# Moving 21 first-matrix tiles and 26 gathered rows ahead of the second-matrix stage, and splitting more tiles

## The chip, the cores and the metric

The kernel is one inference step of a small hybrid encoder, written for one Trainium2 chip and run on one of its cores. The metric is the device time in microseconds (us) of one execution. A core has engines that each run their own instruction queue strictly in order: TensorE (PE) multiplies matrices, VectorE (DVE) and ScalarE (ACT) do elementwise work, GpSimd (POOL) does elementwise work and starts indexed gathers, and SyncE (SP) starts the plain transfers. Sixteen DMA engines move the data of both kinds of transfers.

## What is computed

The reference runs one layer for two groups of tokens: 256 prompt tokens and 8 sequences of 16 sample tokens, 384 in all, each a row of 1024 numbers. Most of the layer (a modulated norm, an RWKV-7 branch, a sparse attention branch, gates) is done when the change begins to matter. Its last part is a product-key expert layer:

```python
x = x + g2 * _peer(h2, w_pq, peer_keys, peer_u, peer_v)

# inside _peer, for each block of 128 tokens hb:
q = (hb @ w_pq).reshape(128, 8, 2, 64)
s = einsum('nhpd,hpkd->nhpk', q, peer_keys)
...                                  # per head: 16 of 16384 experts e, softmax weights g
act = gelu(einsum('nhkd,nd->nhk', peer_u[e], hb))
return einsum('nhk,nhkd->nd', g * act, peer_v[e])
```

So each token picks 8 x 16 = 128 of 16384 experts. An expert has a row of `peer_u` and a row of `peer_v`, both of 1024 float32 numbers.

## The kernel before

The expert layer is computed in two ways at once, since they need different engines.

**The matrix way, for the 256 prompt tokens.** The 16384 experts are 128 tiles of 128. For each tile j, `dense_u(j)` (L1427) loads a 512 KB tile of `peer_u` (transposed; called `in_puT` in the profile), multiplies it with the tokens into the PSUM tile `fx`, and ACT writes the gelu of it: one late result of 128 x 256 numbers (128 KB). `dense_v(j)` (L1450) loads the 512 KB tile of `peer_v` (`in_pv`) and multiplies the weighted late result with it, adding into four PSUM banks (`bx`, `cp`, and two `dx`). In between, every late result must be multiplied by the tokens' expert weights, a matrix that is zero for the experts that a token did not pick. The stage that builds this matrix is `weights` (L1343): 2 x 32 steps, in each of which DVE and ACT make one-hot factors (`oh`), TensorE multiplies them four times, and the product is multiplied into tiles 0 to 75 where they lie (`G` and `G2`, L1367; DVE in one step, POOL in the next) while its columns for tiles 76 to 127 go to DRAM (`wst`, L1368, L1370) and come back later as `Ws` (L1484).

**Splitting.** A float32 product is either done whole on the float32 data, or as three products of parts: ACT rounds the tile to a high part (`wh`), DVE subtracts to get the low part (`wl`), and TensorE multiplies high x high, high x low, low x high. This is `split` (L1419) and `hilo` (L225). The u tiles 0 to 35 are whole, the others split. In the v stage every third tile is whole (L1453), and a split one also needs its late result split into `Gh` and `Gl`.

**The gather way, for the 128 sample tokens.** `peer_sparse` (L1508) is a Python generator. POOL gathers 128 rows (one per token, 512 KB in all) of `peer_u` or `peer_v` into one of five `raw` buffers (L1518). DVE multiplies a u gather with the tokens and sums (L1529), or adds a v gather times its coefficient to `acc` (L1539). The groups are 4 u gathers, one gelu, 4 v gathers; 256 gathers in all. Each call of `pull(rate)` adds `rate` to a counter and issues two gathers for each whole number in it; in the v stage a gather also waits for the v tile five places earlier (L1660, L1520).

**Order.** The stages follow in program text: whole u tiles, then split u tiles up to 75, then `weights` with `ahead` called after each of its 64 steps, then the loop over the 128 v tiles. A scheduling pass then fixes the order of instructions on each engine; nothing is reordered at run time. Tiles 76 to 127 have no place of their own in the kept results: the first NB of them are written to DRAM (`gO`, L1447) and loaded back (`gB`, two buffers, L1458) when their v tile comes; the others stay in NA = 12 buffers (`gA`). What is not yet done when the v stage begins is done inside it (L1662).

```python
N1, NW, NA, NB = 36, 76, 12, 20                          # L180
SR, UR = (0.5, 0.4, 0.69), 0.5                           # L181
def ahead(n):                                            # L1636
    un[0] += UR
    if todo and un[0] >= 1 and (todo[0] < NW + NB or todo[0] < NW + NB + NA - 1):
        un[0] -= 1
        u = todo.pop(0)
        gs[u] = self.dense_u(u)
    pull(SR[1])
order = sorted(range(128), key=lambda j: (j + 0.5) / NW if j < NW else (j - NW + 0.5) / (128 - NW) + 0.06)
for n, j in enumerate(order):                            # L1659
    pull(SR[2])
    while todo and sum(u >= NW + NB for u in gs) < NA - 1:
        u = todo.pop(0)
        gs[u] = self.dense_u(u)
    self.dense_v(j, gs.pop(j) if j >= NW else self.kept(j), out, n)
```

The key of `order` spreads tiles 76 to 127 evenly among the others. All tiles of `peer_u` and `peer_v`, `Ws`, and `gB` are loaded by SP's queue, in its order; the `w` tiles have four buffers, `wh` four, `wl` three.

Of the kernel before, what the change touches and what calls it, by code (L numbers as in the profile page):

```python
# [176 lines left out]
ORDER = "GGIRRDMMMGRMRDMRGMGGMRMDGMMRRMGDMMMGGGGGGMGGM"  # L177


N1, NW, NA, NB = 36, 76, 12, 20  # L180
SR, UR = (0.5, 0.4, 0.69), 0.5  # L181
S0, PH = 30, 4
WB, EB = (4, 4, 3), 5
UENG, VENG, GENG, VN = 'v', 'v', 'g', 3
SENG = 'gv'
HENG, EENG, OB = 'va', 'vg', 3

# [1510 lines left out]
```

## Time and profile before

| | |
|---|---|
| median of 3 runs | 1863.67 us (1856.91 to 1869.19) |
| profiled execution: its time, its span | 1860.99 us, 1859.2 us |
| mean granted TensorE clock | 0.96 |
| TensorE busy | 1740.9 us (94%) |
| VectorE busy | 1379.4 us (74%) |
| ScalarE, GpSimd busy | 693.3 us (37%), 724.1 us (39%) |
| moved by DMA | 434.11 MB, mean 233 GB/s |

From the trace: the last split u tile of `G2` ends at about 1219 us, the steps of `weights` run from there to about 1364 us, the first v product starts at 1361 us, and the last v product ends at about 1850 us. The rest is the residual and its store.

In the windows quoted below a row gives a stretch of the span, then for PE, PE's weight loads, DVE, ACT and POOL the busy time and in brackets the number of instructions, then the granted clock, the busy share of the DMA engines, and what they moved in GB/s. Group rows read: line, engine, operation, output<-input, size, count | busy time, mean ns of one | idle time before them and what ended it. A float32 product appears as two PE records, one of the split parts as one. Wait rows read: engine and line, what it waited for, total us, times, longest us.

### The profile page before, as it was taken

The page shows a single profiled execution, that of the slowest core. Times are in us where ns is not written, and L with a number is a line of the kernel's source. Part 1 is how long each engine was busy: PE and PEld are TensorE (multiplying, and loading weights), DVE is VectorE, ACT ScalarE, POOL GpSimd, SP SyncE. Part 2 cuts the span into 40 slices and gives each one's busy share as a digit, 9 for nine tenths or more (in the row PEclk, how much of TensorE's full clock was granted, in tenths as well). Part 3 has the DMA queues.
Part 4 walks back from the last instruction along what each step waited for, and adds up shares of the span by engine and source line. Part 5 has one row for each costly group of instructions (what it writes and reads, how often), then busy time and mean ns, then how long its engine had stood idle before and what let it go on. Part 6 is the DMA issues. An engine that isn't in the chain of part 4 may idle for free. (4 is left out here: it accounts for less than half of the span.)

```text
span 1859.2 us, 33617 instructions
## 1 busy us (share of the span) xinstructions
PE 1740.9 (94%) x12621; PEld 1436.3 (77%) x12621; DVE 1379.4 (74%) x2905; ACT 693.3 (37%) x1402; POOL 724.1 (39%) x763
## 2 busy tenths in 40 slices
PE   7997999999999989899988979999999888999998
PEld 4985888877877867798877869999975556776765
DVE  4549678767767745445999999899967777787773
ACT  4432333333243333334221135478842222333332
POOL 2331333223223210024255566563346676465541
PEclk8996999999999989899998989999999999999999
DMA  8421563454264274655487969975489999999994
GB/s 307 141 79 34 168 224 91 147 168 137 78 218 137 70 243 151 213 174 179 148 313 284 359 244 331 383 291 182 164 294 369 375 374 356 351 373 344 347 344 157
DMA packets 181083, 434.11 MB, mean 233 GB/s; under 512 B 39348, under 2 KB 78388, under 8 KB 180920
## 3 DMA queue, kind: packets, MB, share of 16 engines
q1 hardware_dynamic: 144056, 297.73, 46.8%
q0 software_dynamic: 36864, 134.23, 19.3%
q8 instruction: 99, 1.62, 0.3%
q14 instruction: 64, 0.52, 0.1%
HBM read 401.65 MB, written 30.24 MB: 232 GB/s over the span
## 5 line engine op out<-in xcount | busy, mean ns | idle before, releaser
L231 DVE TENSOR_TENSOR wl<-w,wh 128x1024 fp32r<-128x1024 f32 x278 | 351.2, 1269 | 138.5 <-PE mm L223 64.3
L227 ACT ACTIVATE wh<-w 128x1024 fp32r<-128x1024 f32 x282 | 295.3, 1053 | 221.6 <-PE mm L223 88.0
L223 PE MATMUL fx<-h2h,wl 128*128 128x256 f32 x736 | 214.3, 291 | 10.4 <-DVE wl L231 10.3
L1518 POOL DMA_INDIRECT raw<-in_pu,pe x128 | 161.9, 1265 | 154.5 <-DVE acc L1539 46.6
L223 PE MATMUL fx<-h2h,wh 128*128 128x256 f32 x736 | 215.6, 293 | 4.3 <-ACT wh L227 3.2
L1518 POOL DMA_INDIRECT raw<-in_pv,pe x128 | 169.8, 1327 | 121.0 <-PE dx L223 45.4
L223 PE MATMUL fx<-h2l,wh 128*128 128x256 f32 x736 | 209.8, 285 | 0.0
L1539 DVE SCALAR_TENSOR_TENSOR acc<-raw,dots,acc 128x1024 f32<-128x1024 f32 x127 | 169.8, 1337 | 17.9 <-DMA raw<-in_pv,pe 16.7
L1529 DVE SCALAR_TENSOR_TENSOR raw<-raw,sh 128x1024 f32<-128x1024 f32 x128 | 163.4, 1291 | 17.1 <-DMA raw<-in_pu,pe 16.7
L223 PEld LDWEIGHTS fx<-h2h,wl 128*128 128x128 f32 x736 | 140.1, 190 | 14.4 <-DVE wl L231 12.7
L223 PEld LDWEIGHTS fx<-h2h,wh 128*128 128x128 f32 x736 | 140.9, 191 | 10.1 <-ACT wh L227 4.5
L223 PE MATMUL fx<-h2f,w 128*128 128x256 f32 x576 | 133.5, 394 | 14.4 <-ACT G L1445 14.4
L223 PEld LDWEIGHTS fx<-h2l,wh 128*128 128x128 f32 x736 | 140.4, 191 | 2.1 <-issue 1.7
L223 PEld LDWEIGHTS fx<-h2f,w 128*128 128x128 f32 x576 | 112.9, 198 | 33.3 <-ACT G L1445 16.4
L223 PE MATMUL mm<-LTh,wh 128*128 128x384 f32 (+1 forms) x344 | 121.9, 355 | 1.7 <-ACT wh L227 1.0
L223 PE MATMUL mm<-LTl,wh 128*128 128x384 f32 (+1 forms) x344 | 120.7, 351 | 1.2 <-POOL LTl L477 1.2
L223 PE MATMUL mm<-LTh,wl 128*128 128x384 f32 (+1 forms) x344 | 121.0, 352 | 0.0
L223 PE MATMUL mm<-wh,LTh 128*128 128x256 f32 (+1 forms) x360 | 105.4, 293 | 0.6 <-ACT qx L876 0.6
L223 PE MATMUL mm<-wh,LTl 128*128 128x256 f32 (+1 forms) x360 | 104.6, 291 | 0.0
L223 PE MATMUL mm<-wl,LTh 128*128 128x256 f32 (+1 forms) x360 | 104.4, 290 | 0.0
L1367 POOL TENSOR_TENSOR G<-G,wg 128x144 f32<-128x144 f32 (+1 forms) x64 | 61.7, 988 | 85.6 <-ACT wg L1364 85.5
L223 PEld LDWEIGHTS mm<-wh,LTh 128*128 128x128 f32 x360 | 70.1, 195 | 4.6 <-issue 2.7
(549 smaller groups left out, 4193.3 us busy)
## 6 DMA issues: line engine op xcount, KB each, us to landing
w<-in_puT SPq DMA_DIRECT2D x128, 512.0 KB, 6.1
w<-in_pv SPq DMA_DIRECT2D x128, 512.0 KB, 6.8
w<-in_w_in SPq DMA_DIRECT2D x70, 512.0 KB, 4.5
w<-in_w_ada SPq DMA_DIRECT2D x48, 512.0 KB, 4.2
cKT<-in_cKT SPq DMA_DIRECT2D x32, 256.0 KB, 4.2
cV<-in_cV SPq DMA_DIRECT2D x32, 256.0 KB, 4.5
w<-in_w_pq SPq DMA_DIRECT2D x16, 512.0 KB, 3.6
d<-wst SPq DMA_DIRECT2D x8, 832.0 KB, 4.3
```

What stands on the lines that cost most here:

```text
L223: return self.nc.tensor.matmul(out, l, r, start=start, stop=stop, skip_group_check=True, **kw)
L227: self.nc.scalar.activation(hi, src, AF.Copy)
L231: (self.nc.vector if eng == "v" else self.nc.gpsimd).tensor_tensor(lo, src, hi, op=OP.subtract)
L1367: (nc.vector if w is p else nc.gpsimd).tensor_tensor(g, g, w[:, :, c0:c1], op=OP.mult)
L1518: d = nc.gpsimd.indirect_dma_start(out=u, out_offset=None, in_=src, in_offset=bass.IndirectOffsetOnAxis(ap=e[:, j:j + 1], axis=0))
L1529: nc.vector.scalar_tensor_tensor(u, u, 1.0, h2, op0=OP.mult, op1=OP.mult, accum_out=dots[:, j:j + 1])
L1539: nc.vector.scalar_tensor_tensor(acc, v, dots[:, j:j + 1], acc, op0=OP.mult, op1=OP.add)
```

## The change

Only tables of numbers change:

```diff
-N1, NW, NA, NB = 36, 76, 12, 20
-SR, UR = (0.5, 0.4, 0.69), 0.5
+N1, NW, NA, NB = 36, 76, 12, 41
+SR, UR = (0.5, 0.62, 0.55), 0.82
 S0, PH = 30, 4
 WB, EB = (4, 4, 3), 5
-UENG, VENG, GENG, VN = 'v', 'v', 'g', 3
+UENG, VENG, GENG, VN = 'v', 'v', 'g', 5
```

`UR` is the rate at which `ahead` takes up u tiles: 64 steps x 0.5 = 32, of which the limit in `ahead` lets 31 through; 64 x 0.82 = 52.48, so all 52. `NB` = 41 sends 41 of the 52 late results through DRAM and leaves 11 in the `gA` buffers. `SR[1]` and `SR[2]` are the rates of `pull` beside the steps of the matrix and beside the v tiles: 26 more gathers now stand in the weights stage, and as many fewer in the v stage. `VN` = 5 makes every fifth v tile whole: 26 whole tiles, not 42, so 16 more are split.

The order of the instructions, read from the built programs. First VectorE in the weights stage, from the 1841st row of its queue on. `wl` is the low part of a u tile, `oh` the one-hot factors, `G` the kept results multiplied by the matrix, `acc` and `raw` the work on gathered rows. Before:

```order
L1539 SCALAR_TENSOR_TENSOR acc_11650<-raw_15415,dots_15338,acc_11650 128x1024
L1354 TENSOR_TENSOR oh_13568<-wA_13431,wB_13432 128x512
L1402 TENSOR_TENSOR oh_13568<-pT_2137_11034,dx_13148 128x512
L231 TENSOR_TENSOR wl_13468<-w_13464,wh_13467 128x1024
L1367 TENSOR_TENSOR G_11261<-G_11261,mm_13509 128x4x36
L1367 TENSOR_TENSOR G_2273_11729<-G_2273_11729,mm_13509 128x4x40
L1354 TENSOR_TENSOR oh_13585<-wA_13431,wB_13432 128x512
L1539 SCALAR_TENSOR_TENSOR acc_11650<-raw_15418,dots_15338,acc_11650 128x1024
L231 TENSOR_TENSOR wl_13538<-w_13534,wh_13537 128x1024
```

The same place now:

```order
L1539 SCALAR_TENSOR_TENSOR acc_11650<-raw_15339,dots_15115,acc_11650 128x1024
L1354 TENSOR_TENSOR oh_13689<-wA_13507,wB_13508 128x512
L1402 TENSOR_TENSOR oh_13689<-pT_2137_11034,dx_13148 128x512
L231 TENSOR_TENSOR wl_13416<-w_13412,wh_13415 128x1024
L1529 SCALAR_TENSOR_TENSOR raw_15449,dots_15448<-raw_15449,sh_2254_11648 128x1024
L1367 TENSOR_TENSOR G_11261<-G_11261,mm_13624 128x4x36
L1367 TENSOR_TENSOR G_2273_11729<-G_2273_11729,mm_13624 128x4x40
L1354 TENSOR_TENSOR oh_13742<-wA_13507,wB_13508 128x512
L1539 SCALAR_TENSOR_TENSOR acc_11650<-raw_15342,dots_15115,acc_11650 128x1024
L231 TENSOR_TENSOR wl_13476<-w_13472,wh_13475 128x1024
L1529 SCALAR_TENSOR_TENSOR raw_15452,dots_15448<-raw_15452,sh_2254_11648 128x1024
```

Rows of `raw` work stand between the steps where there were none. In the whole stage from its 1823rd row to the first `Gl`, VectorE had 4 rows of `acc` and none of `raw`, with 33 of `wl`; now it has 16 of `acc`, 14 of `raw` and 54 of `wl` (three of each `wl` count belong to the first v tiles). The gathered rows all lie in the first 30 of the 62 rows that multiply `G`; the later part holds one-hot factors and `wl` alone.

Second, SP's queue in the later part of the v stage. `w` is a loaded tile, `Ws` four tiles' columns of the weight matrix, `gB` a late result from DRAM. Before, from row 717:

```order
L1484 DMA Ws_18571<-d_11262 128x8x128
L1416 DMA w_17459<-in_puT 128x1024
L1416 DMA w_17492<-in_pv 128x1024
L1416 DMA w_17521<-in_pv 128x1024
L1416 DMA w_17527<-in_pv 128x1024
L1416 DMA w_17556<-in_puT 128x1024
L1416 DMA w_17589<-in_pv 128x1024
L1416 DMA w_17619<-in_pv 128x1024
L1416 DMA w_17628<-in_puT 128x1024
```

Now, from row 733:

```order
L1484 DMA Ws_17916<-d_11262 128x8x128
L1416 DMA w_17643<-in_pv 128x1024
L1458 DMA gB_17746<-d_11263 128x256
L1416 DMA w_17671<-in_pv 128x1024
L1416 DMA w_17698<-in_pv 128x1024
L1416 DMA w_17712<-in_pv 128x1024
L1458 DMA gB_17800<-d_11263 128x256
L1416 DMA w_17740<-in_pv 128x1024
L1416 DMA w_17765<-in_pv 128x1024
```

The 512 KB loads of u tiles are gone from this stretch, and 128 KB loads of late results stand there instead. No u tile is left in SP's queue, or in TensorE's, after the first v product. Ahead of the weights stage, up to the 1845th row of VectorE's queue, the kinds of instructions stand in the same order as before.

## The prediction

> **What bounds the kernel now.** I read the stretches of the last stages first, then the prices of single instructions, the waits of the queues, and last what the DMA engines moved. The rows are the end of the split u tiles, the weights stage, three parts of the v stage, and below them a stretch inside the weights stage.
>
> ```profile
> span 1859.2 us, 33617 instructions
> 1100.00:1219.00 119.00, 116.51 (x959) 115.11 (x960) 109.95 (x138) 58.61 (x105) 69.35 (x47) 1.00 0.95 357
> 1219.00:1364.00 145.00, 142.88 (x1213) 141.64 (x1211) 136.59 (x207) 124.98 (x299) 59.45 (x62) 1.00 0.55 194
> 1364.00:1550.00 186.00, 166.48 (x554) 106.64 (x554) 137.13 (x174) 47.05 (x77) 120.16 (x102) 0.96 0.99 370
> 1550.00:1800.00 250.00, 242.96 (x1140) 182.38 (x1141) 191.26 (x237) 86.76 (x132) 134.05 (x104) 0.99 0.95 353
> 1800.00:1850.00 50.00, 50.00 (x185) 34.45 (x183) 25.81 (x31) 16.31 (x26) 5.07 (x4) 1.00 0.63 213
> 1255.00:1273.00 18.00, 18.00 (x157) 18.00 (x156) 17.50 (x28) 15.86 (x39) 6.79 (x8) 1.00 0.50 175
> ```
>
> In the weights stage TensorE never pauses (18.00 of 18.00) and VectorE hardly does; the DMA engines are half idle. The v stage, 486 us, has two halves. Up to 1550 it has no u tile; the DMA engines are full (0.99, 370 GB/s) and TensorE waits. From 1550 on the 21 u tiles come in, TensorE is busy 97% and the DMA engines 95%. So the change takes work from a stage limited by loads, then by loads and TensorE together, and puts it into one limited by TensorE and VectorE.
>
> **Prices on TensorE.** Pieces of the chain that ended last, with start, length and count of records; here they follow each other without a gap:
>
> ```profile
> 1576.73 2.88 PE fx L223 x24
> 1572.38 0.92 PE dx L223 x4
> 1715.16 0.86 PE cp L223 x2
> 1716.02 1.72 PE dx L223 x4
> ```
>
> A u tile is 24 records of 0.12 us, 2.88 us. A split v tile is 12 records of 0.23 (0.92 / 4), 2.76 us. A whole one is 8 records of 0.43, 3.44 us. A one-hot record comes out of the 18 us row: the order puts 64 of them beside eight steps, so 157 records are 64 and 93 of u tiles; 18.00 - 93 x 0.12 = 6.84, / 64 = 0.107, and a product has two.
>
> **The change, stage by stage.** *Weights stage.* TensorE gets 21 u tiles, 21 x 2.88 = +60.5 us, and there was no gap to take them. That is the lower bound. VectorE gets 21 `wl` and 26 gathered rows, and the order (above) puts those rows into the first half of the stage, where VectorE will be late and TensorE will wait; after the last of them TensorE still has many u tiles to do alone. Groups of VectorE in the weights stage, then three of the stretch 1150 to 1219, where gathers run:
>
> ```profile
> L231 DVE TENSOR_TENSOR wl<-w,wh 128x1024 fp32r<-128x1024 f32 x34 | 45.3, 1334 | 6.2 <-ACT oh L1407 2.8 <-ACT wst L1368 1.1 <-issue 1.0
> L1354 DVE TENSOR_TENSOR oh<-wA,wB 128x512 f32<-128x512 f32 x55 | 38.7, 729 | 0.1
> L1367 DVE TENSOR_TENSOR G<-G,mm 128x160 f32<-128x160 f32 (+1 forms) x62 | 27.2, 481 | 0.0
> L1402 DVE TENSOR_TENSOR oh<-pT,dx 128x512 f32<-128x512 f32 x27 | 18.3, 679 | 0.0
> L1539 DVE SCALAR_TENSOR_TENSOR acc<-raw,dots,acc 128x1024 f32<-128x1024 f32 x4 | 5.4, 1352 | 0.0
> L1394 DVE TENSOR_TENSOR wB<-wab,clate 128x512 bf16<-128x512 bf16 x6 | 4.5, 758 | 0.0
> L1393 DVE TENSOR_TENSOR wA<-wA,pT 128x256 f32<-128x256 f32 x6 | 3.7, 621 | 0.0
> L1391 DVE TENSOR_TENSOR wA<-wab,clate 128x256 f32<-128x256 bf16 x6 | 2.8, 466 | 0.1
> ...
> L1539 DVE SCALAR_TENSOR_TENSOR acc<-raw,dots,acc 128x1024 f32<-128x1024 f32 x14 | 18.0, 1285 | 1.8 <-DMA raw<-in_pv,pe 1.6
> L1529 DVE SCALAR_TENSOR_TENSOR raw<-raw,sh 128x1024 f32<-128x1024 f32 x15 | 17.8, 1219 | 1.8 <-DMA raw<-in_pu,pe 1.8
> L1529 DVE DVE_READ_ACCUMULATOR raw<-raw,sh 128x1 f32 x14 | 1.1, 82 | 0.0
> ```
>
> I follow VectorE from its 1823rd row (the first multiplication of `G` after the last split u tile) to its 1972nd, a `wl` soon after the last gathered row, and from there TensorE. Busy time by count: 34 `G` at 0.439 (27.2 / 62) 14.9, 29 `oh` at 0.704 20.4, 14 at 0.678 9.5, 26 `wl` at 1.332 34.6, 16 `acc` at 1.286 20.6, 14 `raw` at 1.27 (1.19 and 0.08 to read the sum) 17.7, 17 small ones at about 0.5, 8.6; together 126 us. The groups overlap a little: the eight groups shown and 3 us of smaller ones add to 149 us where the window says 136.6 busy, a factor of 0.916, which leaves 116 us. Behind that `wl` TensorE still has 622 records of u tiles and 108 one-hot products, 622 x 0.12 + 108 x 0.213 = 97.6 us. The path is 213 us. Before, the same start gives 3.5 us for a first `wl` and then TensorE throughout, 718 x 0.12 + 220 x 0.213 = 133 us, 136.5 us.
>
> ```profile
> 1220.10 0.94 DVE L1367 TENSOR_TENSOR G<-G,mm 128x160 f32<-128x160 f32 x2
> L223 PE MATMUL bx<-w,G x52: 590/591/669, 1361.2 to 1827.3; 128*128 128x512 f32 x52
> ```
>
> From that start to the first v product it took 141 us, 3% more. So **+77 us**, with the 3% **+79**; I take +78. It can't be below +60.5; above, the landing of rows may show. In the v stage VectorE waited this long for rows, 65 of them:
>
> ```profile
> DVE raw L1529 <- DMA raw<-in_pu,pe: 10.7, 4, 3.5
> DVE acc L1539 <- DMA raw<-in_pv,pe: 5.7, 4, 3.8
> ```
>
> (16.4 us in 186, so 26 rows at that price are 7 us), and each group of four stops VectorE for a gelu by ACT, which is busy 125 of 145 us here; with twice those 7 us the upper end is +92.
>
> Taken at nothing in this stage: 21 more stores of late results on SP, 21 `wh` and 21 gelus on ACT, 26 gathers on POOL.
>
> ```profile
> SPq L1447 <- ACT gO L1445: 45.2, 17, 4.7
> POOL G L1367 <- ACT wg L1364: 85.5, 27, 9.5
> L227 ACT ACTIVATE wh<-w 128x1024 fp32r<-128x1024 f32 x34 | 36.2, 1065 | 6.0 <-PE fx L223 4.4 <-DMA w<-in_pv 1.4
> L1445 ACT ACTIVATE gO<-fx 128x256 f32<-128x256 f32 x20 | 7.7, 384 | 0.0
> L1518 POOL DMA_INDIRECT raw<-in_pv,pe x16 | 23.6, 1477 | 13.7 <-DVE raw L1529 8.8 <-issue 3.0 <-DVE acc L1539 1.8
> ```
>
> SP waits on a store for its gelu, 2.7 us at a time (45.2 / 17), and the next u loads stand behind it; four `w` buffers and half-idle DMA engines cover that. If they did not, 21 x 2.7 = 57 us would be at stake, but 20 such stores cost TensorE nothing that shows in the 18.00 row. ACT goes from 125 to about 155 us (21 x 1.45) in a stage that grows to over 215; POOL's 85.5 us of idle time holds 26 gathers of 1.5 us.
>
> *v stage.* What the DMA engines moved from 1364 to 1850, with its issues, then from 1364 to 1550, and one of VectorE's groups from 1364 to 1850:
>
> ```profile
> DMA packets 59818, 167.54 MB, mean 345 GB/s; under 512 B 5361, under 2 KB 21233, under 8 KB 59790
> w<-in_puT SPq DMA_DIRECT2D x21, 512.0 KB, 6.9
> gB<-d SPq DMA_DIRECT2D x20, 128.0 KB, 7.1
> raw<-in_pu,pe POOLq DMA_INDIRECT x76, 8.0
> raw<-in_pv,pe POOLq DMA_INDIRECT x76, 8.0
> DMA packets 28896, 68.73 MB, mean 370 GB/s; under 512 B 2329, under 2 KB 13994, under 8 KB 28887
> L231 DVE TENSOR_TENSOR Gl<-gA,Gh 128x256 fp32r<-128x256 f32 x22 | 9.3, 422 | 14.9 <-ACT Gh L227 14.8
> ```
>
> 21 u tiles and 26 gathers of 0.524 MB go, 24.6 MB; 21 late results of 0.131 MB come, 2.8 MB: 145.7 MB remain. TensorE loses 60.5 us of u tiles and 16 x (3.44 - 2.76) = 11 us by splitting, and has 26 x 3.44 + 102 x 2.76 = 371 us left. VectorE had 137 + 191 + 26 = 354 us; 26 gathered rows (at 1.28) and 21 `wl` (at the 1.33 above) go, 16 `wl` and 16 `Gl` (0.42 each) come: about 320. So the loads are the longest, as in the first half. At its 370 GB/s, all but the last five tiles and the results (3.1 MB) take 142.6 / 0.370 = 385 us; some ten split tiles are then still to be multiplied, 28 us. 413 us, **-73**. Bounds: at the 353 GB/s of the second half 404 + 28 = 432, -54; if loads never bound, TensorE at the 0.96 clock of the first half, 371 / 0.96 = 386 and about 4 us to the first product, -96. I take the first half's rate, since the stage now has its mix throughout: gathers, v tiles and late results, no u tile.
>
> The Trainium skill ("DMA: Bandwidth & Descriptors", section "Where 436 GB/s comes from") has two ceilings: about 358 GB/s for a core's transfers from HBM, and 435 for the fabric of the on-chip memory. By the one the stage would take 142.6 / 0.358 + 28 = 426 us and save 60, which ends at 1882, the edge of my forecast's own range; by the other TensorE would bind, which is rival B. The measured 370 GB/s over 186 us lies above the first and far from the second, so I take neither.
>
> *Sum*: +78 - 73 = **+5 us** on the profiled 1861 us, 1866. The median of the runs shown is 2.7 us above the profiled execution; so I forecast **1868 us**, no change that counts: a measurement of this kernel can tell about 1% (19 us).
>
> **The rivals.**
>
> *A, slower: late results come too late.* A reloaded late result must land (7.1 us), be multiplied by POOL behind its gathers, and only then can ACT round it; ACT's queue has the next tiles' `wh` behind that.
>
> ```profile
> ACT Gh L227 <- POOL gB L1464: 39.1, 9, 7.6
> L1464 POOL TENSOR_TENSOR gB<-gB,Ws 128x256 f32<-128x256 f32 x20 | 20.2, 1015 | 2.1 <-DMA modr<-d 1.4 <-DVE raw L1529 0.4
> ```
>
> 20 of them cost ACT 39.1 us; 21 more at the same price, uncovered, are +41, so 1868 + 41 = 1909. Against it: these 39.1 us lie in the 186 us where the DMA engines were full anyway. They came one per 9.3 us there and will come one per about 8 (41 over some 105 tiles of 3.2 us). With two buffers it decides once one result holds its buffer for over 16 us; landing, multiplying and the `Gl` take 8.5 (7.1 + 1.0 + 0.4), and ACT's part and the queueing would have to add as much again. Chance 0.12.
>
> *B, faster: the v stage becomes TensorE's.* With the u tiles gone the queues may be fed better than at 370 GB/s. Then it saves 90 to 96, and with VectorE keeping up better in the weights stage, +68 (between 60.5 and 78): 1864 + 68 - 93 = 1839. For it, 357 GB/s at 0.95 up to 1219 is 376 at full share; against it, 0.99 is as full as the engines get. Chance 0.12.
>
> *C, slower: the weights stage stumbles.* VectorE, ACT and TensorE are all near full there, and rows that land late stop VectorE in its order: +92, with the v stage as forecast, 1864 + 92 - 73 = 1883. Chance 0.10.
>
> That the change does not do what it says is ruled out by the order, which has no u tile after the first v product.
>
> **How the numbers follow.** My forecast has 0.66, with its own range of 1852 to 1882. Faster by over 1% (below 1845): B, 0.12. Slower by over 1% (above 1882): A, most of C, 0.20. Within 1%: the rest, 0.68. The range must leave out no more than 0.2: it takes in B and C and leaves out A, 1840 to 1890.
>
> **What would show it.** In the profile after: the stretch from the first row after 1219 to the first v product some 220 us long, with TensorE pausing in its first half, not in its second; from there to the end of the products about 413 us, DMA share 0.97 or more nearly to the end, and TensorE near 90% throughout. A stage of 205 us would show that VectorE's rows cost nothing (towards B). DMA shares of 0.9 in the v stage, with ACT waiting on POOL's `gB` for over 80 us, would be A. The forecast fails if the two stages don't change by nearly the same amount.

## The result, and the profile after

The changed kernel takes 1877.12 us (median of 8 runs, 1872.7 to 1886.76) against 1861.66 us for the kernel before (8 runs): a ratio of 1.0089, 95% interval 1.0067 to 1.011. It is 15 us slower, below the 1% that was called no change, and 9 us above the forecast of 1868. As a change it is +15 us where the forecast had +5: the 1868 us stood on the 1863.67 us that the kernel before had in its first three runs, 2 us above its median here. One of the 12 runs of experiment 5 was slow, 1880.52 us; the median there has it in, the ratio leaves it out.

The same starts and ends as in the prediction, read in the timeline: from VectorE's first multiplication of `G` after the last split u tile to the first v product, and from there to the end of the last v product. In after the three instructions are (start, length, engine, line, operation):

```profile
1220.34 0.93 DVE L1367 TENSOR_TENSOR G<-G,mm 128x160 f32<-128x160 f32 x2
...
1442.87 1.02 PE L223 MATMUL bx<-w,G 128*128 128x512 f32 x2
...
1866.19 0.63 PE L223 MATMUL dx<-wh,Gl 128*128 128x512 f32 x2
```

| | weights stage | v stage | sum |
|---|---|---|---|
| before | 141 | 489 | 630 |
| forecast | 220 | 413 | 633 |
| after | 222.5 | 424 | 646.5 |

So the change put 81.5 us into the first stage (forecast 78) and took 65 out of the second (forecast 73). The prediction counted the v stage of before from 1364 us on, 486 us; from the first v product, as here, it is 489, so that its 413 us would be 76 less, and its two stages together +3, not +5. The profiled execution of after took 1876.63 us, 15.6 more than that of before.

The first line of the page of after:

```profile
span 1874.7 us, 33942 instructions
```

Stretches of the last stages of after, with the columns as before (PE, PEld, DVE, ACT, POOL, granted clock, DMA share, GB/s); the first two are the weights stage in halves, the next three the v stage while it is loaded, in halves and whole, the last its end:

```profile
1219.00:1325.00 106.00, 93.94 (x759) 92.46 (x758) 104.60 (x148) 70.86 (x159) 68.63 (x57) 0.97 0.88 314
1325.00:1443.00 118.00, 114.92 (x962) 114.75 (x961) 85.67 (x124) 83.68 (x185) 21.40 (x32) 0.99 0.54 185
1443.00:1630.00 187.00, 173.78 (x641) 119.66 (x639) 149.17 (x185) 62.45 (x98) 105.82 (x84) 0.99 0.98 363
1630.00:1820.00 190.00, 171.50 (x623) 118.54 (x624) 157.90 (x188) 63.73 (x98) 110.92 (x92) 0.97 0.96 351
1443.00:1820.00 377.00, 345.29 (x1264) 238.20 (x1263) 307.07 (x372) 126.18 (x195) 216.74 (x175) 0.98 0.97 357
1820.00:1866.00 46.00, 45.90 (x177) 32.75 (x176) 29.95 (x39) 17.47 (x27) 7.55 (x6) 1.00 0.70 252
```

The weights stage has two unlike halves now. In the first VectorE is full (104.60 of 106) and TensorE pauses for 12 us; in the second TensorE pauses for 3 us and VectorE for 32. Three groups of VectorE over the whole stage, from 1219 to 1443, suggest why:

```profile
L231 DVE TENSOR_TENSOR wl<-w,wh 128x1024 fp32r<-128x1024 f32 x54 | 68.2, 1264 | 30.2 <-issue 15.2 <-ACT oh L1407 8.0 <-ACT wst L1368 3.7
...
L1539 DVE SCALAR_TENSOR_TENSOR acc<-raw,dots,acc 128x1024 f32<-128x1024 f32 x16 | 21.0, 1315 | 0.1
L1529 DVE SCALAR_TENSOR_TENSOR raw<-raw,sh 128x1024 f32<-128x1024 f32 x15 | 19.0, 1273 | 0.0
```

The gathered rows (`acc` and `raw`, 40 us) have no idle time before them: VectorE went from one to the next. In the v stage the DMA engines are at 0.97, not 0.99, and move 357 GB/s, not the 370 that the forecast took. What they moved from 1443 to 1866, and three waits from 1443 to 1820 (who, for whom, total us, times, longest):

```profile
DMA packets 56219, 146.13 MB, mean 345 GB/s; under 512 B 4961, under 2 KB 23521, under 8 KB 56195
```

```profile
PEld bx L223 <- ACT wh L227: 31.7, 21, 3.8
...
ACT Gh L227 <- POOL gB L1464: 23.5, 7, 5.9
PE bx L223 <- ACT wh L227: 23.1, 18, 3.4
```

The bytes are as forecast (145.7 MB). ACT waits for late results, 23.5 us in all, with the next tile's `wh` queued behind, and TensorE waits 23.1 us for `wh`. Whether one causes the other, and both the lower rate, is what the experiments had to say.

### The profile page after: what moved, and what is told of

Read it like the earlier page. It is cut to its first block, busy times and chain, and to the rows that moved or that the text cites. A ratio compares the mean times of both kernels' runs of the same rounds, so it can differ in the third digit from the quotient of the medians.

```text
span 1874.7 us, 33942 instructions
## 1 busy us (share of the span) xinstructions
PE 1742.6 (93%) x12685; PEld 1451.3 (77%) x12685; DVE 1410.6 (75%) x2937; ACT 716.9 (38%) x1434; POOL 729.4 (39%) x763
## 5 line engine op out<-in xcount | busy, mean ns | idle before, releaser
L231 DVE TENSOR_TENSOR wl<-w,wh 128x1024 fp32r<-128x1024 f32 x294 | 373.4, 1275 | 138.6 <-PE mm L223 60.5
L227 ACT ACTIVATE wh<-w 128x1024 fp32r<-128x1024 f32 x298 | 311.3, 1054 | 200.9 <-PE mm L223 82.3
L1518 POOL DMA_INDIRECT raw<-in_pu,pe x128 | 166.4, 1300 | 184.0 <-PE dx L223 69.0
L1367 POOL TENSOR_TENSOR G<-G,wg 128x144 f32<-128x144 f32 (+1 forms) x64 | 54.8, 879 | 103.8 <-ACT wg L1364 103.5
L227 ACT ACTIVATE Gh<-G 128x256 fp32r<-128x256 f32 x62 | 25.8, 418 | 130.1 <-PE dx L223 118.2
```

The source lines that it names most:

```text
L227: self.nc.scalar.activation(hi, src, AF.Copy)
L231: (self.nc.vector if eng == "v" else self.nc.gpsimd).tensor_tensor(lo, src, hi, op=OP.subtract)
L1367: (nc.vector if w is p else nc.gpsimd).tensor_tensor(g, g, w[:, :, c0:c1], op=OP.mult)
L1518: d = nc.gpsimd.indirect_dma_start(out=u, out_offset=None, in_=src, in_offset=bass.IndirectOffsetOnAxis(ap=e[:, j:j + 1], axis=0))
```

## The experiments

Theories at the start: the 20 us of the weights stage beyond its u tiles come from the rows standing bunched, so spreading them or taking them away returns them; and 357 GB/s is what this mix of loads gives, so that late results do not limit the v stage. The rival to the second was that the 10 us missing in the v stage are rival A at a fraction of its price, the rate being held down by gaps. Ratios are to the kernel before, run on the same chip.

**1. The rows spread.** In the changed kernel, each of the last 26 gathers of the weights stage waits for a one-hot product of its own, evenly over 56 of the 64 steps:

```diff
...
+        if self.pace is None and self.rows > 54:
+            return self.steps[min(len(self.steps) - 1, 4 + (self.rows - 54) * 56 // 26)]
...
```

The rest of the edit notes the products of each step and counts the gathers.

> The changed kernel with its gathers in the weights stage spread evenly over the 64 steps instead of lying in the first half (each late one waits for the products of a step that is chosen for it); the same instructions otherwise. Theory (bunched rows make VectorE late in the first half and leave TensorE alone in the second): the stretch from 1220 us to the first v product falls from 222 to 203-210 us, near the 60.5 us of TensorE work alone over the 141 of before; total about 1860-1866, 12 to 17 us under the changed kernel. Rival (any gathered row costs VectorE time that nothing hides, wherever it lies; or POOL's waits now hold up its multiplications): stretch 218-230, total 1873 or more.

1872.63 us, 1.007 (1.0039 to 1.0101): not the 1860 to 1866 of the theory, and an interval that overlaps after's. Weights stage 210.5 us, at the upper edge of the theory's 203 to 210, v stage 433. The two halves of its weights stage:

```profile
1220.00:1325.00 105.00, 102.64 (x865) 101.87 (x864) 92.60 (x130) 76.37 (x171) 41.57 (x43) 1.00 0.78 261
1325.00:1431.00 106.00, 101.69 (x848) 100.00 (x847) 93.93 (x134) 73.44 (x171) 46.56 (x47) 1.00 0.73 247
```

The halves are alike, TensorE pauses 2 us in the first (it was 12) and 4 in the second, and the stage is 12 us shorter. But the v stage gave 9 back, most of it right at its start. TensorE's and ACT's timelines there (start, length, engine, line, operation, and in brackets the idle time before with what ended it):

```profile
1431.01 1.02 PE L223 MATMUL bx<-w,G 128*128 128x512 f32 x2
...
1434.42 1.98 PE L223 MATMUL dx<-w,G 128*128 128x512 f32 x4 [1.54 <-POOL G L1367]
1441.62 0.79 PE L223 MATMUL bx<-wh,Gh 128*128 128x512 f32 x1 [5.22 <-ACT Gh L227]
```

```profile
1441.15 0.72 ACT L227 ACTIVATE Gh<-G 128x256 fp32r<-128x256 f32 x2 [8.74 <-DMA d<-wst]
```

and the same step of ACT in after:

```profile
1446.58 0.73 ACT L227 ACTIVATE Gh<-G 128x256 fp32r<-128x256 f32 x2 [2.30 <-DMA d<-wst]
```

The first whole v tile waits for POOL's last `G`, which stands behind gathers, and ACT's first `Gh` waits 8.7 us for the store of the last `wst`; in after this was 2.3 us. From the end of ACT's last copy into `wst` to this first `Gh` it is 11.7 us here, 5.3 in after. That the store lands later because the gathers share the DMA engines with it (a share of 0.73 here, of 0.54 in after) is likely, and not shown by itself. Either way, spreading right to the end of the stage moved part of the cost to the hand-over.

**2. The rows taken back.** `SR` as before, the u tiles still all in the weights stage:

```diff
-SR, UR = (0.5, 0.62, 0.55), 0.82
+SR, UR = (0.5, 0.4, 0.69), 0.82
```

> The changed kernel with the old gather rates 0.4 and 0.69: all u tiles still ahead of the v stage, but 26 gathers back in the v stage. Theory (v stage bound by loads at about 357 GB/s, weights stage bound by TensorE without the rows): weights stretch 201-206 us, v stage 423 + 13.6 MB / 0.357 = 461; total 1877 - 18 + 38 = 1897. Rival (the v stage is bound by something else than bytes, such as late results or splitting): v stage 425-440, total 1860-1875.

1881.23 us, 1.0105 (1.0064 to 1.0146). Weights stage 202.3 us, v stage 445.4. The first is as the theory had it; the second and the total lie between the theory (461 and 1897) and the rival (at most 440 and 1875). Its weights stage in halves, then the loaded part of its v stage:

```profile
1219.00:1325.00 106.00, 104.75 (x888) 104.35 (x887) 84.47 (x124) 80.20 (x176) 28.66 (x32) 1.00 0.67 224
1325.00:1422.00 97.00, 97.00 (x826) 96.98 (x825) 69.83 (x103) 72.38 (x165) 22.15 (x32) 1.00 0.55 180
1422.00:1820.00 398.00, 354.16 (x1273) 240.75 (x1271) 332.95 (x414) 127.42 (x200) 256.83 (x199) 0.97 1.00 372
```

This takes the change apart. The 21 u tiles alone cost the weights stage 202.3 - 141.1 = 61 us, the 60.5 of the prediction's lower bound, with TensorE full in its second half (97.00 of 97), and free, with the 16 tiles more that are split, 489 - 445.4 = 44 of the v stage. The 26 rows then cost 20 more in the weights stage and free 21 in the v stage. Of the 20, 14 are pauses of TensorE (15.1 us over the stage in after, 1.3 here). The other 6 are slower products: the 1707 records of the stage keep TensorE busy 207.4 us in after, at a granted clock of 0.98, and 201.1 us here, at 1.00. With all rows back, the DMA engines run at 372 GB/s and a share of 1.00: more than after's 357, from the same kind of loads.

**3. Every third tile whole again**, in the changed kernel:

```diff
-UENG, VENG, GENG, VN = 'v', 'v', 'g', 5
+UENG, VENG, GENG, VN = 'v', 'v', 'g', 3
```

> The changed kernel with every third v tile whole, as before. Theory (v stage bound by loads): 11 us more on TensorE, 28 us less on VectorE, most of both hidden; total within -3 to +7 us of the changed kernel's 1877. Rival (VectorE at 81% and its order hold the v stage up, so splitting cost what the stage fell short of the forecast): 7 to 15 us faster, 1862-1870.

1875.24 us, 1.0074 (1.0033 to 1.0114), weights stage 222.7, v stage 421. Its loaded part:

```profile
1443.00:1820.00 377.00, 354.96 (x1228) 229.34 (x1227) 273.50 (x348) 106.81 (x166) 195.37 (x177) 0.99 0.98 362
```

TensorE is busy 9.7 us more and VectorE 33.6 us less than in after, and the time is the same, as the theory had it. In the changed kernel the splitting costs and brings nothing that can be measured. ACT's wait for late results is nearly three times that of after (23.5):

```profile
ACT Gh L227 <- POOL gB L1464: 66.2, 20, 8.0
```

Yet the stage is 3 us shorter. So the sum of these waits does not say what late results cost.

**4. Four buffers for late results**, in the changed kernel:

```diff
-            g = self.t([128, 256], tag="gB", bufs=2)
+            g = self.t([128, 256], tag="gB", bufs=4)
```

> The changed kernel with four buffers for reloaded late results, not two. Theory (late results are not what limits the v stage): within 3 us of the changed kernel's 1877. Rival A (late results come too late, ACT waits on POOL's multiplication): the 23.5 us that ACT waits there go mostly, 8 us or more faster.

1868.51 us, 1.0051 (1.0027 to 1.0075), the rival. Weights stage 222.6 as in after, v stage 414. Its loaded part and its waits from 1442 to 1810:

```profile
1442.00:1810.00 368.00, 342.41 (x1270) 237.21 (x1269) 306.24 (x374) 126.64 (x197) 220.16 (x175) 0.99 0.99 366
```

```profile
PE bx L223 <- ACT wh L227: 16.7, 14, 2.4
...
ACT Gh L227 <- POOL gB L1464: 3.7, 1, 3.7
```

ACT's wait for late results falls from 23.5 to 3.7 us, TensorE's for `wh` from 23.1 to 16.7, the rate rises from 357 to 366 GB/s, and the stage loses 10 us: it is the 413 of the forecast. 10 us over 41 late results is 0.24 us each, where rival A had 2. In the medians the step is 8.6 us; the two intervals just overlap. That the buffers raise the rate is what this pair shows. That they do it by way of ACT's wait is not shown: experiment 3 has more of that wait than after, and no loss.

**5. The same four buffers in the kernel before** (the edit of experiment 4):

> The kernel before with four buffers for reloaded late results. It tells whether the 8 to 10 us of the four buffers are a cost that the change brought, or one the kernel had. Theory (a cost of the change: 20 results in a stretch with full DMA engines, 0.99, waited without harm; 41 in a leaner stage do not): within 3 us of before, 1859-1865. Rival (each late result costs about 0.25 us wherever it is): 20 x 0.25 = 5 us faster, 1855-1858.

1857.71 us, 0.9974 (0.9948 to 1.0), where the rival had it. The weights stage stays at 141.6; the v stage goes from 489 to 484. The stretch that the prediction called full anyway, and ACT's wait in it:

```profile
1362.00:1550.00 188.00, 169.89 (x585) 108.84 (x585) 145.57 (x182) 51.39 (x82) 127.92 (x103) 0.98 1.00 379
```

```profile
ACT Gh L227 <- POOL gB L1464: 6.6, 3, 3.4
```

A DMA share of 0.99 at 370 GB/s became 1.00 at 379, and ACT's wait fell from 39.1 to 6.6 us. By these two traces the two buffers cost the kernel before some 5 us of its v stage, a quarter of a microsecond for each of the 20 late results. The interval reaches 1.0, so the medians alone leave the gain open.

**6. Both repairs in the changed kernel**: four buffers, and the rows spread over 44 steps, not 56, so that the last gathers end some 16 steps before the hand-over:

```diff
...
+            return self.steps[min(len(self.steps) - 1, 4 + (self.rows - 54) * 44 // 26)]
...
```

> The changed kernel with both repairs: gathers of the weights stage spread over its first 48 steps, so that the last multiplications of POOL don't stand behind them, and four buffers for late results. Theory (the two costs lie in different stages and add): weights stretch 208-213 us, v stage 412-418 with no pause at its start; total 1877 - 10 - 9 = 1858, 1854-1862, level with before. Rival (the repairs overlap, or the gap at the hand-over comes back): 1864-1870.

1857.05 us, 0.9972 (0.9953 to 0.999): as the theory had it, and faster than both kernels, by 0.3% against the one before. Weights stage 212.8, v stage 417.4. Both stages in its trace, then ACT's first `Gh` and TensorE's first v tile:

```profile
1230.00:1443.00 213.00, 203.95 (x1708) 201.56 (x1708) 192.76 (x269) 150.03 (x342) 99.09 (x90) 1.00 0.77 257
1443.00:1820.00 377.00, 348.12 (x1294) 240.72 (x1293) 309.14 (x379) 127.97 (x198) 216.66 (x177) 0.99 0.98 363
```

```profile
1447.41 0.72 ACT L227 ACTIVATE Gh<-G 128x256 fp32r<-128x256 f32 x2 [2.43 <-DMA d<-wst]
```

```profile
1443.57 1.02 PE L223 MATMUL bx<-w,G 128*128 128x512 f32 x2
...
1445.28 1.88 PE L223 MATMUL dx<-w,G 128*128 128x512 f32 x4
1447.88 0.50 PE L223 MATMUL bx<-wh,Gh 128*128 128x512 f32 x1 [0.72 <-ACT Gh L227]
```

The hand-over is as short as in after (2.43 us; the first split tile 4.3 us after the first whole one), and the 10 us of bunching stay saved. (Its profiled execution, 1870.64 us, reached the weights stage 10 us late, which has nothing to do with these stages.) But experiment 5 has the same time, 1857.71, without the change: repaired, the change itself is worth nothing that these intervals, 0.2 to 0.3% to each side, can show. The two stages do not favour it either: 630 us here, 625 in experiment 5, one trace each.

**7. Late u tiles mixed over the v stage.** In the kernel before, another 20 late results go to DRAM: not the first 20 of the 52, but every 2.6th. Kept results are then used from the start of the v stage on, buffers come free, and the 21 tiles whose u half runs in the v stage are spread over it, not gathered in its second part. There are two `gB` buffers as before:

```diff
-SR, UR = (0.5, 0.4, 0.69), 0.5
+SR, UR, OFF = (0.5, 0.4, 0.69), 0.5, [NW + k for k in range(52) if (k + 1) * NB // 52 > k * NB // 52]
...
-        off = NW <= j < NW + NB
+        off = j in OFF
...
```

> The kernel before with another choice of which 20 late results go to DRAM: every 2.6th of the 52, not the first 20. Then kept results are used from the start of the v stage on, buffers come free, and the 21 u tiles of the v stage lie between its tile 7 and about 86, not all behind tile 50. Theory (before, the first part of the v stage is bound by loads with TensorE at 90%, the second by TensorE with the DMA engines at 95%; mixing evens both): v stage 489 to 470-480, total 1845-1855. Rival (both are full nearly everywhere and only the order changes): 1858-1866.

1864.19 us, 0.9994 (0.9975 to 1.0013): no gain; v stage 491.5. Two of its stretches:

```profile
1450.00:1550.00 100.00, 95.36 (x415) 67.86 (x416) 79.78 (x98) 32.80 (x51) 58.05 (x48) 1.00 0.99 373
1550.00:1650.00 100.00, 95.37 (x423) 70.33 (x422) 77.64 (x95) 32.62 (x49) 50.28 (x43) 0.97 0.98 356
```

TensorE is busy 95 of 100 us and the DMA engines 98% in both. The theory that a half limited by loads and a half limited by TensorE could be averaged into something shorter fell: by this run, before's v stage has no slack of that kind left to even out.

**8. The splitting alone, in the kernel before** (`VN` from 3 to 5):

> The kernel before with every fifth v tile whole and nothing else of the change. Theory (splitting relieves TensorE by 0.68 us a tile, which counts only behind tile 50, where TensorE binds): 9 tiles there, 6 us, so 1854-1860. Rival (VectorE's 1.75 us for each of 16 more tiles counts): 5 us or more slower, 1867 or more.

1864.02 us, 1.001 (0.9995 to 1.0025), v stage 488; neither the gain nor the loss that was expected. Its second part:

```profile
1550.00:1800.00 250.00, 238.05 (x1164) 185.03 (x1165) 209.21 (x257) 96.49 (x149) 137.99 (x108) 0.99 0.97 359
```

TensorE is busy 238.05 of 250 us, before 242.96; the DMA share rose from 0.95 to 0.97. A likely reason for the missing gain is that this part, with the u tiles in it, is bound by both, so that taking work from TensorE leaves the loads. Ahead of it, from 1365 to 1550, the loads ran at 361 GB/s and a share of 0.98, where before had 370 and 0.99; why is open.

**9. Rows back and four buffers** (the edits of experiments 2 and 4):

> The changed kernel with the old gather rates and four buffers for late results. With the old rates and two buffers the v stage already had a DMA share of 1.00 at 372 GB/s. Theory (waits for late results cost time only where they leave the loads idle): within 4 us of the same kernel with two buffers, 1877-1885. Rival (each of the 41 results costs about 0.2 us wherever it is): 8 us or more faster, 1873 or less.

1878.76 us, 1.0093 (1.006 to 1.0125), weights stage 202.3, v stage 445. Its loaded part and ACT's wait there:

```profile
1422.00:1820.00 398.00, 352.63 (x1276) 237.97 (x1275) 334.53 (x413) 126.41 (x199) 254.04 (x199) 0.98 0.99 370
```

```profile
ACT Gh L227 <- POOL gB L1464: 6.1, 2, 3.1
```

ACT's wait fell from 14.6 us (experiment 2) to 6.1, and the stage did not change, 445 us in both, as the theory had it. So four buffers bring nothing where the loads run without a gap already (372 and 370 GB/s); in after, whose DMA share was 0.97, they do.

**10. Half way.** The kernel before with four buffers, 30 late results, and rates between the two kernels:

```diff
-N1, NW, NA, NB = 36, 76, 12, 20
-SR, UR = (0.5, 0.4, 0.69), 0.5
+N1, NW, NA, NB = 36, 76, 12, 30
+SR, UR = (0.5, 0.5, 0.62), 0.66
```

(and `VN` = 4)

> Half of the change with four buffers for late results: 30 late results through DRAM, 41 u tiles ahead of the v stage and 11 in it, gather rates 0.5 and 0.62, every fourth v tile whole. Theory (what leaves the v stage comes back in the weights stage one for one, so the time is flat between the two kernels once late results don't wait): 1855-1861, as the kernel before with four buffers (1858). Rival (the two stages each have one engine full, and a point between them evens both out): 1852 or less.

1868.15 us, 1.0039 (1.002 to 1.0058), slower than the theory and the rival had it. Weights stage 184 us, v stage 449. Its weights stage in two parts:

```profile
1219.00:1300.00 81.00, 70.43 (x565) 69.29 (x564) 75.92 (x107) 54.41 (x122) 39.10 (x35) 0.96 0.79 276
1300.00:1403.00 103.00, 103.00 (x881) 103.00 (x881) 84.76 (x133) 83.13 (x196) 27.46 (x38) 1.00 0.51 179
```

141 and ten u tiles of 2.88 are 170. Of the 14 above, 10.6 are TensorE's pauses in the first part. So the cost of bunching does not fall away with a smaller move: 14 rows cost 14 us here, 26 cost 20 in after.

**11. Half way, rows spread** over 44 steps as in experiment 6:

> The kernel of the half-way run (30 late results, four buffers for them), with its gathered rows spread evenly over the first 48 steps of the weights stage instead of bunched at its start. The theory: the half-way run's weights stage took 184 us, 141 of before and 10 u tiles by 2.88 = 29 make 170, and the 14 over it are the bunched rows, in whose stretch TensorE was busy 70 of 81 us. Spread, they cost 1 to 4 us, so the stage takes 171 to 174; the stage of the v tiles keeps its 449, and the time is 1852 to 1858. The rival: VectorE and the gathers on GpSimd run later into the end of the weights stage, and the first v tile waits for them, or the v stage, which is loaded in its first part, takes it back; then the stage's saving shows, but the time is 1862 or more.

1865.75 us, 1.0013 (0.9991 to 1.0035): the rival. Weights stage 177 us, v stage 453. Its weights stage, then TensorE and ACT where the stages meet:

```profile
1222.00:1300.00 78.00, 77.09 (x657) 76.91 (x656) 65.66 (x94) 58.04 (x136) 30.71 (x32) 1.00 0.70 234
1300.00:1400.00 100.00, 95.21 (x795) 94.64 (x794) 93.71 (x140) 75.12 (x180) 45.14 (x44) 0.98 0.66 225
```

```profile
1400.77 1.02 PE L223 MATMUL bx<-w,G 128*128 128x512 f32 x2
1404.89 2.07 PE L223 MATMUL cp<-w,G 128*128 128x512 f32 x2 [3.10 <-ACT wst L1368]
1406.76 3.62 PE L223 MATMUL dx<-w,G 128*128 128x512 f32 x4
1413.71 0.50 PE L223 MATMUL bx<-wh,Gh 128*128 128x512 f32 x1 [3.33 <-ACT Gh L227]
```

```profile
1402.79 1.06 ACT L227 ACTIVATE wh<-w 128x1024 fp32r<-128x1024 f32 x1 [2.55 <-DMA w<-in_pv]
...
1413.24 0.72 ACT L227 ACTIVATE Gh<-G 128x256 fp32r<-128x256 f32 x2 [8.40 <-DMA d<-wst]
```

The bunching is gone (77.09 of 78), but the first split v tile starts 12.9 us after the first whole one; in experiment 6 it was 4.3. ACT's last copies stand behind a `wh` that waits 2.55 us for its v tile, the store of the last `wst` starts late, and the first `Gh` waits for it, 8.4 us after the end of the last copy (5.3 in experiment 10). In the sum of the two stages (630 us; 633 in experiment 10) some 3 of the 7 us are left.

## Why the prediction was right, and where it was not

**What bounds.** The weights stage was TensorE's, with VectorE close behind, as read from the 18.00 row: experiment 2 adds 61 us for 21 u tiles and nothing else. The v stage was limited by loads, then by loads and TensorE together: experiments 3, 7 and 8 shift, add or take TensorE's work there and the time stays, which fits this reading.

**Weights stage, +78.** It measured +81.5, between the bounds. The mechanism was the one named: VectorE late with rows in the first half, TensorE alone at the end. Taking the rows away gives 20 us back (experiment 2), spreading them 12 (experiment 1), 10 with the buffers (6). The path from VectorE's row counts to the remaining TensorE work, 220 us with its 3%, was 2.5 us short. VectorE took 118 us to the end of that `wl` (forecast 116), and TensorE then 104.4, not 97.6: it had 656 records of u tiles and 116 one-hot products left, not 622 and 108.

**Taken at nothing.** SP's 21 more stores, ACT's work and POOL's gathers did not show in the stretch: experiment 2 has the stores and ACT's work, and costs no more than the u tiles. POOL's gathers do cost something if they run up to the hand-over (experiments 1 and 11), which the prediction did not see; in after they do not.

**v stage, -73.** It measured -65, inside the bounds of -54 and -96. The step that failed is "I take the first half's rate": the rate was 357 GB/s and not 370, which makes 142.6 / 0.357 = 399 us of the 385. The bytes were right. The 28 us behind them were some 24: the 142.6 MB had landed at about 1843 us (142.35 MB at 1842), and the last product ended at 1866.8. So two terms were off, by +14 and by -4, and 399 + 24 = 423 stands against 424 measured. With four buffers 142.6 / 0.366 + 24 is 414, as measured.

**Rival A** pointed at the right buffers at eight times their price, and so was put aside whole when it should have been a small term of the sum. Its own sign, ACT waiting on `gB` for over 80 us, did not come: 23.5. The sign itself was a poor one: 66.2 us of it in experiment 3 went with no loss. But the argument against it, that before's 39.1 us lie "where the DMA engines were full anyway", does not hold as it stands: the same stretch went from 370 to 379 GB/s with more buffers (experiment 5). So 0.99 was not "as full as the engines get", as the prediction put it against rival B. With the old gather rates, at 370 to 372 GB/s, two more buffers brought nothing (2 and 9); why they did in the one case and not in the other is open.

**The ceiling at 358.** The Trainium skill ("DMA: Bandwidth & Descriptors", section "Where 436 GB/s comes from") puts a core's transfers from HBM at about 358 GB/s, which gave an end at 1882. After's 357 GB/s seems to bear that out, and is no evidence for it: the same kinds of loads ran at 366, 372 and 379 GB/s over 188 to 398 us in experiments 4, 2 and 5. What held the rate at 357 was gaps: at its share of 0.97 it is 368 at a full share, and 366 at 0.99 in experiment 4 is 370.

**Rivals B and C** did not come. TensorE was busy 345.29 of 377 us in the v stage, and the weights stage stayed 10 us below C's +92.

## What to carry to other kernels

Work moved out of a stage bound by two things at once can give back less than it costs where it goes: 21 u tiles cost 61 us of a full TensorE and freed 44. Work that is added to a stage for a second engine should be spread over the stage, or that engine is late in one half and idle in the other; and it should end some way before the hand-over to the next stage. Before a busy share of 0.99 is taken for full, give the waiting queue more buffers and see whether the rate moves: it did in experiment 5, and did not in experiment 9. The sum of an engine's waits is no price: experiment 3 had 66.2 us of them and lost nothing.

## What the runs showed of the hardware

A short pause of TensorE can cost more than itself. In experiment 11 it paused for 3.1 us ahead of the product at 1404.89, and the records behind ran at half speed: four took 3.62 us where the same four take 1.88 in experiment 6. The windows of 4 us there:

```profile
1400.00:1404.00 4.00, 1.79 (x11) 0.96 (x9) 2.37 (x3) 1.45 (x3) 2.73 (x4) 1.00 0.59 208
1404.00:1408.00 4.00, 3.11 (x4) 1.51 (x5) 1.44 (x2) 0.84 (x3) 1.17 (x2) 0.50 0.79 206
```

The granted clock went from 1.00 to 0.50. The Trainium skill ("TensorE: Matmul & The Clock Gate", section "Part 1: The HAM clock gate") has the half rate after an idle window of about 3.4 us; the rate agrees, and a pause of 3.1 us was enough here. In experiment 10 one of 2.84 us, ahead of the product at 1412.13, was enough too: the clock granted from 1412 to 1416 was 0.62.

Gathers, 512 KB loads and 128 KB reloads together ran at up to 379 GB/s over 188 us (experiment 5).
